# A two-layer encoder on one core: the banded heads' product with the low part of the keys over 128 rows, and where its room comes from

## The chip, the core and the metric

The kernel runs on one core of one Trainium2 chip. Its time is the device time of one execution in microseconds. TensorE (PE) multiplies, VectorE (DVE), ScalarE (ACT) and GpSimd (POOL) do the elementwise work, and SyncE (SP) issues the loads and stores.

## What is computed

An encoder of two layers over 512 tokens of width 1024, in float32. Each layer mixes tokens with three groups of heads (differential, latent, banded), attends to 256 memory tokens, and ends in a SwiGLU block; each part is normalised before and after. Cut to what matters here:

```python
for l in range(DEPTH):
    h = rmsnorm(x, g_mix_pre[l])
    (a_q, a_k, a_v, b_cq, b_ckv, b_kr, c_q, c_k, c_v) = jnp.split(h @ w_in[l], IN_SPLITS, axis=-1)
    ...
    qb = (rmsnorm(b_cq, mla_q_norm_g[l]) @ mla_w_q_up[l]).reshape(B, S, MLA_HEADS, MLA_NOPE + MLA_ROPE)
    qb = jnp.concatenate([qb[..., :MLA_NOPE], rope(qb[..., MLA_NOPE:], positions)], axis=-1)
    ...
    o_c = swa_attention(c_q.reshape(B, S, SWA_Q_HEADS, HEAD_DIM), c_k..., c_v...,
                        positions, swa_slopes, swa_sinks[l])
    mix = jnp.concatenate([o_a, o_b, o_c], axis=-1) @ w_out[l]
    x = x + rmsnorm(mix, g_mix_post[l])
    xo = cross_attention(rmsnorm(x, g_x_pre[l]), rmsnorm(mem, g_x_mem[l]), w_xq[l], w_xkv[l], w_xo[l])
```

In the banded heads (`swa_attention`) a tile of 128 queries sees its own 128 keys and the tile before and after. There are 8 query heads of 64 columns over 2 key heads.

## The kernel before, in words

Products keep nearly full float32 accuracy by splitting each operand into a high and a low part (`split`, L100 to L102: a copy that rounds on ScalarE, the remainder on VectorE) and adding three products, high by high, low by high, high by low (`mm3`, L145 to L149).

The program is written down as two streams that are woven together. The main stream is the attention in units of one head and one query tile: 16 units of differential heads, 32 of banded ones, 16 of latent ones (`chunk_units`, `diff_units`, `swa_units`, `mla_units`). Each unit is a list of stages: a score, a softmax, transposes of the weights, products with the values. The fill stream supplies TensorE with products that don't depend on attention (`fill` in `mix_phase`). Its steps there are, in the order of the string `FILL_ORDER = "qqummummukkkuu"`: "q" query columns of the banded heads, "u" one token tile of the latent heads' queries and keys (`mla_up`, with `products` and, one step later, `transposed`), "m" half a step of a memory tile's norm (`mem_norm`: load, squares, scaling; then the transposes), "k" a product of the memory with its key weights (`make_xK`). Numbers in tables set how much fill stands beside each stage. A scheduler then orders the instructions of each engine; on the chip every engine keeps that order.

The banded heads' scores are taken at L690 and L691. Keys of both key heads stand in one tile `KScV`: plane 0 and plane 1 hold the high part of head 0 and of head 1, copied to both halves of the 128 rows, and plane 2 holds the low parts, head 0 in rows 0 to 63 and head 1 in rows 64 to 127. A query tile `SQ` holds the high part in one half of the rows and the low part in the other. So L690 gives (high + low of the query) by the high part of the key in one product of 128 rows, and L691 adds the high part of the query by the low part of the key, over 64 rows. A score has 256 or 384 columns (the band is cut off at the ends).

Temporary tiles come from rings, one for each tag; `TMP_BUFS` says how many buffers a ring has. A tile that is asked for takes the next buffer of its ring, and its first writer waits for the last reader of the tile that had it. Tag "o" (2 buffers) has, around the change, the transposed values' source `cvT`, the two halves of each memory tile (L1041 loads them), and the tiles `t` in which products of the memory are collected before they are stored to DRAM (L1061). Tag "m" (3 buffers) has `qn` and `kn`, the latent heads' queries and keys of one token tile, `r5b5`, in which the rotary step of that tile is computed (L744 to L757), and the latents' norms (`latent_T`).

The memory tiles go this way: load (L1041 on SP's queue), squares on ScalarE (L199), the root on GpSimd (L203, L204), scaling on VectorE (L216), transposes on TensorE into `ps_at` (L180), split into `memTh` and `memTl` (L101, L102). Then `make_xK` multiplies.

Of the kernel before, what the change touches and what calls it, by code (L numbers as in the profile page):

```python
# [18 lines left out]
P = 128  # L19
D = 1024  # L20
KC = 8
S = 512
# [15 lines left out]
TMP_BUFS = {"e": 5, "ph": 2, "pl": 2, "o": 2, "c": 2, "m": 3}  # L38
# [10 lines left out]
def weave(main, fill, ratio):  # L49
    """Alternate the emission of two streams: `ratio` steps of fill for each step of main."""  # L50
    owed = 0.0
    done = object()
    for _ in main:
        owed += ratio
        while owed >= 1.0:
            owed -= 1.0
            if next(fill, done) is done:
                owed = -1e9
    for _ in fill:
        pass  # L60
# [9 lines left out]
def encoder_kernel(  # L70
# [16 lines left out]
    # ---------------------------------------------------------------- helpers  # L87
# [16 lines left out]
    def stage(pieces, a, b):  # L104
        """Weights from DRAM into one staging tile [P, a, b]; pieces: (partition, row chunk, column, source)."""
        st = stp.tile([P, a, b], F32, tag="st", name="st")
        for p0, k0, c, src in pieces:
            n, k, m = src.shape
            nc.sync.dma_start(st[p0:p0 + n, k0:k0 + k, c:c + m], src)
        return st  # L110

    def unit(st_view):
        """Staged weights [P, a, b] as a list of a (high, low) operands [P, b]."""
        a, b = st_view.shape[1], st_view.shape[2]
        per = 512 // b
        out_ = []
        for k0 in range(0, a, per):
            k1 = min(k0 + per, a)
            hi = wp.tile([P, k1 - k0, b], F32R, tag="wh", name="wh")
            lo = wp.tile([P, k1 - k0, b], F32R, tag="wl", name="wl")  # L120
            split(hi, lo, st_view[:, k0:k1, :])
            out_ += [(hi[:, k, :], lo[:, k, :]) for k in range(k1 - k0)]
        return out_
# [8 lines left out]
    def defer(n, i, *fns):  # L132
        """Emit fns, which belong to token tile i, n ticks later."""
        late.extend((ticks[0] + n, i, f) for f in fns)
# [24 lines left out]
    class Split8:  # L159
        """A [P, 8, n] operand as exact high and low parts, in 4-chunk slots."""  # L160
# [15 lines left out]
    def to_T(src_half, dst, half, t0, name):  # L176
        """Transpose a [P, 512] half of a token tile into chunks 4*half.. of dst, split."""
        pt = psum("at")
        for c in range(4):
            nc.tensor.transpose(pt[:, c * P:(c + 1) * P], src_half[:, c * P:(c + 1) * P], ident)  # L180
        ptv = pt.rearrange("p (c t) -> p c t", c=4)
        k0 = 4 * half
        for j in range(4 // min(4, dst.per)):
            w = min(4, dst.per)
            s = (k0 + j * w) // dst.per
            o = (k0 + j * w) % dst.per
            hi = dst.hi[s][:, o:o + w, t0:t0 + P]
            lo = dst.lo[s][:, o:o + w, t0:t0 + P]
            with tc.high_priority(offset=HASTE):
                split(hi, lo, ptv[:, j * w:(j + 1) * w, :])  # L190

    def sq_mean(halves, dst, t0, name):
        """Mean of squares over the 1024 columns given as two halves, plus EPS, to the power -1/2; the squares pass
        through dst's place for the token tile at t0."""
        ms = small(2, name + "ss")
        w = min(4, dst.per)
        for j, hv in enumerate(halves):
            k = 4 * j % dst.per
            nc.scalar.activation(dst.hi[4 * j // dst.per][:, k:k + w, t0:t0 + P],  # L199
                                 hv.rearrange("p (c t) -> p c t", t=P), AF.Square, scale=1.0 / 32.0,  # L200
                                 accum_out=ms[:, j:j + 1])
        r = small(1, name)
        nc.gpsimd.tensor_scalar(out=r, in0=ms[:, 0:1], scalar1=ms[:, 1:2], scalar2=EPS, op0=ALU.add, op1=ALU.add)  # L203
        nc.gpsimd.tensor_tensor(out=r, in0=r, in1=neghalf[:, :1], op=ALU.pow)  # L204
        return r

    def norm_to_T(halves, g, dst, t0, name, hs, spread=False):
        """rmsnorm with gain g into hs; returns the transposes into dst. spread: the first half off the vector engine."""
# [15 lines left out]
    def post_norm(i, a0, a1, g, dst, spread=False):  # L224
        """x += rmsnorm of the two halves a0, a1 with gain g. spread: the first half's gain off the vector engine."""
# [15 lines left out]
    # ---------------------------------------------------------------- setup  # L241
# [35 lines left out]
    cos2 = cp.tile([P, NT, 32], F32, tag="cos2", name="cos2")  # L277
# [15 lines left out]
    def setup():  # L293
# [16 lines left out]
        # positions in exact 16-bit halves, as rows and as columns  # L310
# [19 lines left out]
    def setup_rest():  # L330
# [13 lines left out]
        # rotary angles, reduced to [-pi, pi] by exact products of short pieces  # L344
# [46 lines left out]
        nc.scalar.activation(cos2[:, :, 0:16], cang, AF.Sin)  # L391
        nc.vector.tensor_copy(out=cos2[:, :, 16:32], in_=cos2[:, :, 0:16])
        nc.vector.tensor_scalar(out=sin2[:, :, 0:16], in0=sin2[:, :, 16:32], scalar1=-1.0, scalar2=None, op0=ALU.mult)

    # ---------------------------------------------------------------- pieces of a layer
    def transpose_pair(es, k0, k1):
        """Chunks k0..k1 of two tiles of weights -> split [128 keys, chunk, 2 x 128 queries]."""
        pt = psum("at")
        for k in range(k0, k1):
            for j, e in enumerate(es):  # L400
                c = 2 * (k - k0) + j
                nc.tensor.transpose(pt[:, c * P:(c + 1) * P], e[:, k * P:(k + 1) * P], ident)  # L402
        n = 2 * P * (k1 - k0)
        hi, lo = tmp("ph", (P, n), F32R), tmp("pl", (P, n), F32R)
        split(hi, lo, pt[:, :n])
        return [(hi[:, 2 * P * j:2 * P * (j + 1)], lo[:, 2 * P * j:2 * P * (j + 1)]) for j in range(k1 - k0)]

    def split_v(dst, src):
        """Values of two heads [P, ..., 2, 64] -> [P, ..., high 0, low 0, low 1, high 1]."""
# [3 lines left out]
    def ws_chunk(ps, u, hT, t0, t1):  # L413
        """Weight-stationary product: ps[:, t0:t1] = (128 weight columns).T @ hT[:, t0:t1]."""
# [3 lines left out]
    def as_tile(ps, us, aT, t0, n, ks=tuple(range(KC)), first=True, last=True, ticks_=False):  # L418
        """Activation-stationary product: ps[:, :n] = aT[:, t0:t0+128].T @ weights, over row chunks ks."""
# [6 lines left out]
    def nat_units(w, cols):  # L426
        """Natural-layout weights, all eight row chunks."""
# [41 lines left out]
    # ---------------------------------------------------------------- layers  # L469
# [3 lines left out]
    def mix_phase(l, head):  # L473
# [12 lines left out]
        KS_cV = slot("Sq", [P, 5, S], F32R, "KScV")  # L486
        KS, cV = KS_cV[:, 0:3, :], KS_cV[:, 3:5, :].rearrange("p a (k b d) -> p (a k) b d", b=4, d=64)
# [8 lines left out]
        # ---- projections of the mixing block  # L496
# [13 lines left out]
        def in_swa_kv():  # L510
# [6 lines left out]
            nc.vector.tensor_tensor(out=KS[up, 2, :], in0=ps[up], in1=KS[up, 1, :].bitcast(F32), op=ALU.subtract)  # L517
# [33 lines left out]
        # ---- attention as units of one head and one query tile, each a list of stages  # L551
# [6 lines left out]
        # two units (rows of the same values) share their products with the values; four such units fill half the  # L558
        # rows of an output chunk, eight the chunk
        nop = lambda *a: None  # L560

        def chunk_units(first, soft2, pairs, vals, ends):
            """pairs: per 64-row half, two (unit, unit, key chunks); vals(b, k): stationary values;
            ends: stages on the finished chunk [128, 512]."""
# [43 lines left out]
        def diff_units(c, q3, mdst):  # L608
            """The sums s0 of the first weights stay out of the products: rmsnorm(o / s0) has EPS * s0 ** 2 for EPS."""
# [68 lines left out]
        def swa_units(cp_, ip, mdst):  # L678
            """Heads 2 cp_ and 2 cp_ + 1 of both groups, query tiles 2 ip and 2 ip + 1."""
            def score(u, a, bic):  # L680
                b, i, c = bic
                pr = slice(64 * b, 64 * (b + 1))
# [8 lines left out]
                nc.tensor.matmul(ps[:, :wd], lhsT=q[pr], rhs=KS[pr, 2, c0:c0 + wd], start=False, stop=True)  # L691
# [36 lines left out]
        # ---- latent attention  # L728
        def mla_up(qT, kT, mV):
# [5 lines left out]
            def products(i):  # L735
# [8 lines left out]
                r5b5 = tmp("m", (P, 2, 5, 32))  # L744
# [10 lines left out]
                nc.vector.tensor_tensor(out=r5, in0=r5, in1=cos2[:, i:i + 1, :].to_broadcast([P, 5, 32]), op=ALU.mult)  # L755
# [46 lines left out]
        # ---- emission  # L802
# [37 lines left out]
        def early():  # L840
            """Weights of the steps after this phase, into slots of their own, ahead of the ring."""
# [56 lines left out]
    def latent_T(l, ps, a, n, scale, gl, latT, c0, i):  # L898
        """rmsnorm of ps[:, a:a+n] with gain gl, transposed and split into latT[:, :, c0:..., tile i]."""
# [15 lines left out]
    class Head:  # L915
        """The first products of a layer: the query latents, by token tile, and the first differential heads."""
# [46 lines left out]
    def out_proj(w, aT, wrow, done):  # L963
        """natural = aT.T @ w, by halves of the columns; done(i, half0, half1) takes a finished token tile."""
# [26 lines left out]
    def out_first(w, aT, accs):  # L991
        """First half of the columns of the mixing output, without the latent heads' rows (chunks 2 and 3)."""
# [10 lines left out]
    def out_late(w, aT, st_):  # L1003
        """What is left of the mixing output: st_ takes the weights and the open products of the second half."""
# [77 lines left out]
    def x_attn(l, hT, first):  # L1082
# [44 lines left out]
        def unit_(hd, tp):  # L1127
            """One head, two token tiles."""
# [220 lines left out]
```

## Time and profile before

| | |
|---|---|
| median of 3 runs | 1622.77 us (1622.03 to 1624.49) |
| span of the profiled execution | 1622.5 us |
| TensorE busy | 1579.8 us, 8225 products |
| VectorE busy | 984.2 us |
| ScalarE busy | 806.5 us |
| GpSimd busy | 119.7 us |
| DMA | 167.37 MB, mean 103 GB/s |

The profiled execution's span, from the first to the last instruction, stands for its own time; it lies 0.3 us under the median of the runs. In the page's slices TensorE is at nine tenths or more from the second slice to the last but one, and its granted clock is at full speed in all of them at the page's resolution. A matmul's duration in the trace includes the way through the array, so products in a row overlap; how fast they follow each other is read from their starts. The row "x2" or "x4" merges neighbours of the same kind. A number in brackets behind a row is idle time of that engine just before it, and what ended it.

### The profile page before, as it was taken

To read this page: it belongs to the slowest core of one execution; us is meant where nothing else is said; L and a number is where in the kernel's file an instruction comes from. 1 tells how busy PE (TensorE), PEld (TensorE's weight loads), DVE (VectorE), ACT (ScalarE), POOL (GpSimd) and SP (SyncE) were. 2 spreads that over 40 slices of the span, in tenths; PEclk is the share of its full clock that TensorE was granted. 3 is DMA by queue.
4 is the path that set the end of the run, shared out by engine and by line. 5 is a ranking of instruction groups with operands and counts; after the bars stand their busy time and mean duration, and the time that the engine had idled before them with its cause. 6 is when DMAs were issued, how large, how long until landed. Compare 5 with 4: busy or idle time off the path is not lost.

```text
span 1622.5 us, 21890 instructions
## 1 busy us (share of the span) xinstructions
PE 1579.8 (97%) x8225; PEld 1315.0 (81%) x8225; DVE 984.2 (61%) x1912; ACT 806.5 (50%) x1749; POOL 119.7 (7%) x208
## 2 busy tenths in 40 slices
PE   6999999999999999999999999999999999999998
PEld 6887877799888888888888878777888888888886
DVE  6899776665562554444566987767547434445544
ACT  5578778554553222322356787875445433222222
POOL 3101000300310000000130000003004000000000
PEclk9999999999999999999999999999999999999999
DMA  5632641241233323233245234512312423233221
GB/s 174 153 90 82 204 136 48 77 146 63 78 130 104 104 78 104 78 108 101 89 126 121 68 118 157 162 40 80 129 53 91 142 92 104 78 104 105 78 79 52
DMA packets 130010, 167.37 MB, mean 103 GB/s; under 512 B 21744, under 2 KB 100720, under 8 KB 129136
## 3 DMA queue, kind: packets, MB, share of 16 engines
q1 hardware_dynamic: 129904, 165.97, 32.8%
q8 instruction: 65, 1.06, 0.3%
q14 instruction: 41, 0.34, 0.1%
HBM read 150.22 MB, written 9.44 MB: 98 GB/s over the span
## 4 chain that ended last, share of the span: by engine, by line
PE 90%; DVE 3%; POOL 2%; ACT 2%; issue 1%; DMA 1%; SPq 0%; DVEq 0%; POOLq 0%; ACTq 0%
PE ps_mm L147 14%; PE ps_mm L149 14%; PE ps_mm L148 14%; PE ps_av L149 6%; PE ps_av L148 6%; PE ps_av L147 6%; PE ps_sc L149 5%; PE ps_sc L148 5%; PE ps_sc L147 5%; PE ps_at L402 3%; PE ps_av L573 2%; PE ps_av L574 1%; PE ps_sc L784 1%; PE ps_sc L691 1%; PE ps_at L180 1%
## 5 line engine op out<-in xcount | busy, mean ns | idle before, releaser
L102 DVE TENSOR_TENSOR wl<-st,wh 128x512 fp32r<-128x512 f32 (+1 forms) x406 | 279.4, 700 | 245.6 <-ACT wh L101 242.7
L101 ACT CAST wh<-st 128x512 fp32r<-128x512 f32 (+1 forms) x406 | 243.0, 615 | 304.1 <-PE ps_mm L148 132.6
L149 PE MATMUL ps_mm<-hfh,wl 128*128 128x512 f32 (+1 forms) x384 | 144.5, 376 | 2.5 <-DVE wl L102 2.5
L149 PE MATMUL ps_av<-hfh,wl 128*128 128x512 f32 (+1 forms) x384 | 144.3, 376 | 1.7 <-DVE wl L102 1.7
L147 PE MATMUL ps_mm<-hfh,wh 128*128 128x512 f32 (+1 forms) x384 | 144.4, 376 | 0.6 <-ACT hfh L101 0.6
L148 PE MATMUL ps_mm<-hfl,wh 128*128 128x512 f32 (+1 forms) x384 | 144.6, 377 | 0.0
L147 PE MATMUL ps_av<-hfh,wh 128*128 128x512 f32 (+1 forms) x384 | 144.3, 376 | 0.0
L148 PE MATMUL ps_av<-hfl,wh 128*128 128x512 f32 (+1 forms) x384 | 144.3, 376 | 0.0
L147 PE MATMUL ps_sc<-dwh,f 128*128 128x512 f32 x320 | 124.8, 390 | 0.0
L149 PE MATMUL ps_sc<-dwh,f 128*128 128x512 f32 x320 | 124.6, 389 | 0.0
L148 PE MATMUL ps_sc<-dwl,f 128*128 128x512 f32 x320 | 124.6, 389 | 0.0
L101 ACT CAST dwh<-st 128x1024 fp32r<-128x1024 f32 x40 | 40.0, 1047 | 157.6 <-PE ps_sc L149 153.4
L102 DVE TENSOR_TENSOR pl<-ps_at,ph 128x512 fp32r<-128x512 f32 (+1 forms) x128 | 82.7, 654 | 25.1 <-ACT ph L101 24.1
L149 PEld LDWEIGHTS ps_mm<-hfh,wl 128*128 128x128 f32 x384 | 72.0, 188 | 17.7 <-DVE wl L102 3.0
L149 PEld LDWEIGHTS ps_av<-hfh,wl 128*128 128x128 f32 x384 | 72.0, 187 | 16.8 <-DVE wl L102 2.1
L101 ACT CAST ph<-ps_at 128x512 fp32r<-128x512 f32 (+1 forms) x128 | 70.6, 562 | 29.8 <-PE ps_at L402 28.2
L147 PEld LDWEIGHTS ps_mm<-hfh,wh 128*128 128x128 f32 x384 | 72.0, 187 | 15.7 <-ACT hfh L101 1.1
L148 PEld LDWEIGHTS ps_mm<-hfl,wh 128*128 128x128 f32 x384 | 72.0, 188 | 15.2 <-DVE hfl L102 0.4
L147 PEld LDWEIGHTS ps_av<-hfh,wh 128*128 128x128 f32 x384 | 72.0, 188 | 14.7
L148 PEld LDWEIGHTS ps_av<-hfl,wh 128*128 128x128 f32 x384 | 72.0, 188 | 14.6
L402 PE MATMUL ps_at<-ident,e 128*128 128x128 f32 x480 | 77.2, 275 | 3.3 <-DVE memTl L102 2.2
L203 POOL TENSOR_SCALAR rpost<-rpostss 128x1 f32<-128x1 f32 x24 | 9.0, 375 | 932.0 <-ACT hTh L199 716.1
(363 smaller groups left out, 3896.4 us busy)
## 6 DMA issues: line engine op xcount, KB each, us to landing
st<-in_w_ffn_in SPq DMA_DIRECT2D x44, 1024.0 KB, 5.1
st<-in_w_ffn_out SPq DMA_DIRECT2D x22, 1024.0 KB, 4.9
st<-in_w_xkv SPq DMA_DIRECT2D x16, 1024.0 KB, 5.6
st<-in_w_out SPq DMA_DIRECT2D x16, 512.0 KB, 5.0
st<-in_w_xq SPq DMA_DIRECT2D x8, 1024.0 KB, 5.2
st<-in_w_xo SPq DMA_DIRECT2D x8, 1024.0 KB, 5.4
st<-in_w_in SPq DMA_DIRECT2D x12, 512.0 KB, 4.1
q<-stg SPq DMA_DIRECT2D x48, 128.0 KB, 2.4
```

The costliest lines, as they stand in the source:

```text
L101: nc.scalar.copy(hi, src)
L102: nc.vector.tensor_tensor(out=lo, in0=src, in1=hi.bitcast(F32), op=ALU.subtract)
L147: nc.tensor.matmul(ps, lhsT=lh, rhs=rh, start=first, stop=False)
L148: nc.tensor.matmul(ps, lhsT=lh, rhs=rl, start=False, stop=False)
L149: nc.tensor.matmul(ps, lhsT=ll, rhs=rh, start=False, stop=last)
L180: nc.tensor.transpose(pt[:, c * P:(c + 1) * P], src_half[:, c * P:(c + 1) * P], ident)
L203: nc.gpsimd.tensor_scalar(out=r, in0=ms[:, 0:1], scalar1=ms[:, 1:2], scalar2=EPS, op0=ALU.add, op1=ALU.add)
L402: nc.tensor.transpose(pt[:, c * P:(c + 1) * P], e[:, k * P:(k + 1) * P], ident)
L573: nc.tensor.matmul(av, lhsT=v, rhs=hi, start=k == u["k0"], stop=False)
L574: nc.tensor.matmul(av, lhsT=v, rhs=lo, start=False, stop=k == u["k1"] - 1)
L691: nc.tensor.matmul(ps[:, :wd], lhsT=q[pr], rhs=KS[pr, 2, c0:c0 + wd], start=False, stop=True)
L784: nc.tensor.matmul(ps, lhsT=mla["qT"][:, h, i * P:(i + 1) * P], rhs=mla["kT"][:, h, :], start=True, stop=True)
```

## The change

There are four edits. (1) The low parts of the keys get a plane for each key head, with the other half of the rows zero; `KScV` grows from 5 planes to 6, and GpSimd fills the zero halves in each layer. (2) L691 takes the whole query tile and the key head's plane, all 128 rows. The half of the query tile that holds low parts meets zeros, so the result is the same sum. (3) `r5b5` comes from ring "o" in place of "m", and "m" has 2 buffers in place of 3. (4) The cosine table is kept once, for 16 columns, and read twice by a view. Comments are also removed, which moves line numbers by a few. The core of the diff:

```diff
-TMP_BUFS = {"e": 5, "ph": 2, "pl": 2, "o": 2, "c": 2, "m": 3}
+TMP_BUFS = {"e": 5, "ph": 2, "pl": 2, "o": 2, "c": 2, "m": 2}
...
-    cos2 = cp.tile([P, NT, 32], F32, tag="cos2", name="cos2")
+    cos1 = cp.tile([P, NT, 16], F32, tag="cos1", name="cos1")
...
-        nc.scalar.activation(cos2[:, :, 0:16], cang, AF.Sin)
-        nc.vector.tensor_copy(out=cos2[:, :, 16:32], in_=cos2[:, :, 0:16])
+        nc.scalar.activation(cos1, cang, AF.Sin)
...
-        KS_cV = slot("Sq", [P, 5, S], F32R, "KScV")
-        KS, cV = KS_cV[:, 0:3, :], KS_cV[:, 3:5, :].rearrange("p a (k b d) -> p (a k) b d", b=4, d=64)
+        KS_cV = slot("Sq", [P, 6, S], F32R, "KScV")
+        KS, cV = KS_cV[:, 0:4, :], KS_cV[:, 4:6, :].rearrange("p a (k b d) -> p (a k) b d", b=4, d=64)
...
             nc.vector.tensor_tensor(out=KS[lo, 2, :], in0=ps[lo], in1=KS[lo, 0, :].bitcast(F32), op=ALU.subtract)
-            nc.vector.tensor_tensor(out=KS[up, 2, :], in0=ps[up], in1=KS[up, 1, :].bitcast(F32), op=ALU.subtract)
+            nc.vector.tensor_tensor(out=KS[up, 3, :], in0=ps[up], in1=KS[up, 1, :].bitcast(F32), op=ALU.subtract)
+            nc.gpsimd.memset(KS[up, 2, :].bitcast(F32), 0.0)
+            nc.gpsimd.memset(KS[lo, 3, :].bitcast(F32), 0.0)
...
-                pr = slice(64 * b, 64 * (b + 1))
...
-                nc.tensor.matmul(ps[:, :wd], lhsT=q[pr], rhs=KS[pr, 2, c0:c0 + wd], start=False, stop=True)
+                nc.tensor.matmul(ps[:, :wd], lhsT=q, rhs=KS[:, 2 + b, c0:c0 + wd], start=False, stop=True)
...
-                r5b5 = tmp("m", (P, 2, 5, 32))
+                r5b5 = tmp("o", (P, 2, 5, 32))
...
-                nc.vector.tensor_tensor(out=r5, in0=r5, in1=cos2[:, i:i + 1, :].to_broadcast([P, 5, 32]), op=ALU.mult)
+                r5h = r5.rearrange("p h (a d) -> p h a d", a=2)
+                nc.vector.tensor_tensor(out=r5h, in0=r5h, in1=cos1[:, i:i + 1, :].unsqueeze(1).to_broadcast([P, 5, 2, 16]),
+                                        op=ALU.mult)
```

The scheduler gives some engines another order. SP's queue in the first layer before, from the latent heads' weights to the first store of xK (`in_mem` is the memory, `in_w_xkv` its weights, `gains` a norm's gains):

```order
L109 DMA st<-in_mla_w_q_up 128x2x384
L1041 DMA o<-in_mem 128x512 x2
L923 DMA glat<-in_mla_q_norm_g 128x256
L924 DMA glat<-in_mla_kv_norm_g 128x128
L109 DMA st<-in_mla_w_kv_up 128x512
L109 DMA st<-in_w_xkv 128x8x256
L238 DMA gains<-in_g_x_mem 128x1024
L109 DMA st<-in_w_xkv 128x8x256
L1041 DMA o<-in_mem 128x512 x2
L109 DMA st<-in_w_xkv 128x8x256
L1061 DMA xK_dram<-o 128x512
L109 DMA st<-in_w_xkv 128x8x256
```

and with the change:

```order
L109 DMA st<-in_mla_w_kv_up 128x512
L109 DMA st<-in_w_xkv 128x8x256
L238 DMA gains<-in_g_x_mem 128x1024
L1043 DMA o<-in_mem 128x512
L109 DMA st<-in_w_xkv 128x8x256
L1043 DMA o<-in_mem 128x512 x2
L109 DMA st<-in_w_xkv 128x8x256
L1043 DMA o<-in_mem 128x512
L109 DMA st<-in_w_xkv 128x8x256
L1063 DMA xK_dram<-o 128x512
```

The first memory tile's two halves, which stood together ahead of the weights of the memory, are now further back and apart, and so are the second tile's; the second half of the second tile stands behind the third weight load, and the first store of xK behind the fourth. The queue of the second layer has the same order.

TensorE in the first layer before, around the transposes of the first memory tile (L180; L690 and L691 are score products, L573 and L574 products with the values, L402 transposes of attention weights, L766 those of the latent heads' queries or keys):

```order
L690 MATMUL ps_sc<-KScV,SQ_548 128x256
L691 MATMUL ps_sc<-KScV,SQ_548 128x256
L574 MATMUL ps_av<-pl,aV 128x256
L573 MATMUL ps_av<-ph,aV 128x256
L574 MATMUL ps_av<-pl,aV 128x256
L180 MATMUL ps_at<-ident,o 128x128 x8
L402 MATMUL ps_at<-ident,e 128x128 x4
L766 MATMUL ps_at<-ident,m 96x128 x4
```

and with the change (lines 573 and 574 are now 574 and 575, 402 is 401):

```order
L691 MATMUL ps_sc<-KScV,SQ_548 128x256
L575 MATMUL ps_av<-pl,aV 128x256
L574 MATMUL ps_av<-ph,aV 128x256
L575 MATMUL ps_av<-pl,aV 128x256
L690 MATMUL ps_sc<-KScV,SQ_549 128x256
L691 MATMUL ps_sc<-KScV,SQ_549 128x256
L690 MATMUL ps_sc<-KScV,SQ_548 128x384
L691 MATMUL ps_sc<-KScV,SQ_548 128x384
L180 MATMUL ps_at<-ident,o 128x128 x8
L401 MATMUL ps_at<-ident,e 128x128 x4
```

Two pairs of scores have moved ahead of these transposes. Ahead of the first product with the transposed memory there are nine pairs with the change, and seven before.

## Rows read from the trace of the kernel before

**Rows 1.** The page, busy time, share of the span and instructions of each engine.

```profile
PE 1579.8 (97%) x8225; PEld 1315.0 (81%) x8225; DVE 984.2 (61%) x1912; ACT 806.5 (50%) x1749; POOL 119.7 (7%) x208
```

**Rows 2.** TensorE by line and shape, the 64-row products: count, busy us, mean ns.

```profile
L691 PE MATMUL ps_sc<-KScV,SQ 64*128 64x384 f32 x32 | 14.1, 440 | 0.0
...
L691 PE MATMUL ps_sc<-KScV,SQ 64*128 64x256 f32 x32 | 12.4, 386 | 0.0
```

**Rows 3.** TensorE in order of time: start us, duration us, line, output<-inputs, shape.

```profile
135.56 0.33 PE L690 MATMUL ps_sc<-KScV,SQ 128*128 128x384 f32 x1
135.73 0.40 PE L147 MATMUL ps_mm<-wh,latT 128*128 128x512 f32 x1
135.96 0.40 PE L148 MATMUL ps_mm<-wl,latT 128*128 128x512 f32 x1
136.20 0.39 PE L149 MATMUL ps_mm<-wh,latT 128*128 128x512 f32 x1
136.52 0.44 PE L691 MATMUL ps_sc<-KScV,SQ 64*128 64x384 f32 x1
136.89 0.44 PE L690 MATMUL ps_sc<-KScV,SQ 128*128 128x384 f32 x1
137.25 0.44 PE L691 MATMUL ps_sc<-KScV,SQ 64*128 64x384 f32 x1
137.63 0.55 PE L402 MATMUL ps_at<-ident,e 128*128 128x128 f32 x3
```

**Rows 4.** TensorE in order of time, a 96-row product among 128-row ones.

```profile
97.50 0.39 PE L622 MATMUL ps_sc<-q 96*128 96x512 f32 x1
97.74 0.39 PE L147 MATMUL ps_mm<-hTh,wh 128*128 128x512 f32 x1
```

**Rows 5.** SP's queue in order of time, loads of the memory tiles, first layer.

```profile
98.95 0.96 SPq L1041 DMA_DIRECT2D o<-in_mem  x2
...
142.95 1.05 SPq L1041 DMA_DIRECT2D o<-in_mem  x2
```

**Rows 6.** Landing us: memory loads, then issues of 100 to 200 us (count, KB, median).

```profile
DMA to landing us min/median/max: 2.8/3.2/3.9
...
st<-in_w_xkv SPq DMA_DIRECT2D x8, 1024.0 KB, 5.8
xK_dram<-o SPq DMA_DIRECT2D x4, 256.0 KB, 4.1
```

**Rows 7.** VectorE in order of time, the last adds of two rope steps.

```profile
140.48 0.28 DVE L757 TENSOR_TENSOR m<-m 128x128 f32<-128x128 f32 x1
...
150.46 0.28 DVE L757 TENSOR_TENSOR m<-m 128x128 f32<-128x128 f32 x1
```

**Rows 8.** ScalarE in order of time, the last square of memory tile 1.

```profile
147.19 0.64 ACT L199 ACTIVATE memTh<-o 128x512 fp32r<-128x512 f32 x1
```

**Rows 9.** TensorE in order of time, the memory stage of the first layer.

```profile
142.25 1.35 PE L180 MATMUL ps_at<-ident,o 128*128 128x128 f32 x8 [0.19 <-DVE sr L710]
144.71 0.66 PE L402 MATMUL ps_at<-ident,e 128*128 128x128 f32 x4 [1.11 <-DVE memTl L102]
...
149.92 0.63 PE L180 MATMUL ps_at<-ident,o 128*128 128x128 f32 x4
...
154.63 0.36 PE L147 MATMUL ps_mm<-memTh,wh 128*128 128x256 f32 x1
```

**Rows 10.** TensorE in order of time, first product with the memory, second layer.

```profile
954.50 0.38 PE L147 MATMUL ps_mm<-memTh,wh 128*128 128x256 f32 x1
```

**Rows 11.** Stretches: us; busy us of PE, PEld, DVE, ACT, POOL; granted clock; DMA; GB/s.

```profile
945.00:947.00 2.00, 1.27 (x8) 1.00 (x6) 1.77 (x4) 2.00 (x5) 0.00 (x0) 0.75 0.35 123
947.00:949.00 2.00, 2.00 (x10) 1.77 (x8) 1.49 (x7) 1.53 (x6) 0.89 (x2) 0.50 0.00 0
```

**Rows 12.** GpSimd: a fill by line and shape, and the wait before a gain, layer border.

```profile
masks.py:197 POOL MEMSET ident<- 128x128 f32 x1 | 0.2, 205 | 0.3 <-POOLq L1338 0.3
...
828.59 1.68 POOL L213 TENSOR_TENSOR c<-x,gains 128x512 f32<-128x512 f32 x1 [0.93 <-DVE x L232]
```

## The prediction

> **What bounds the kernel now.** I read the page's busy times first, then TensorE's instructions by shape and in order of time, then the queue of loads, and last who waits around the memory tiles. TensorE is busy in 97% of the span [rows 1], so a microsecond of it that is saved or lost nearly anywhere moves the end. Two places matter, and they pull in opposite directions.
>
> The first is the product that the change is named after. 32 are 384 columns wide and 32 are 256 [rows 2]. Full-height products of 384 and 512 columns follow each other at 0.17 us (135.56 to 135.73) and 0.23 us (135.73 to 135.96) [rows 3]. The 64-row product breaks this rhythm on both sides. Into it: 136.20 to 136.52 is 0.32 instead of 0.23, and 136.89 to 137.25 is 0.36 instead of 0.17. Out of it: 136.52 to 136.89 is 0.37 and 137.25 to 137.63 is 0.38, instead of 0.17. That is 0.29 and 0.40 us lost, 0.345 us on average, at each product. A product of 96 rows in a stream of 128-row ones starts the next after 0.24 us [rows 4], so a shorter contraction alone does not do it; 64 rows do.
>
> The second place is the memory stage, whose work stands in the same stretch. Its first tile is loaded at 98.95 us, long before its transposes at 142.25 us. The second tile is loaded at 142.95 us, when the transposes have freed the buffers "o", and is transposed from 149.92 us [rows 5, 9]. TensorE's order is fixed, so whatever stands behind a transpose waits for it; the products with the transposed memory start at 154.63 us.
>
> **The change, part by part.** *The 64 products.* Columns, output and weights stay; only the height of the operands grows to 128. From the 96-row case I take the plain rhythm for them, so the gain is 0.345 us each, 22 us for 64. The bounds are 0.29 and 0.40 us (18.6 and 25.6 us).
>
> Here a rule speaks against the change. The rows show 0.37 us for a 64-row product where a full one takes 0.17 us [rows 3]. The Trainium skill, page TensorEngine Tiling (Array Packing), section Overview, says instead that a contraction of 64 or less leaves the full array underused and that row tiling may be up to twice as fast, since two half-height tiles can work in parallel. By that rule the widening gives nothing, and the sum below would end 15.9 us higher. The trace does not agree: the neighbours of the half-height products are all full-height, and no two of them overlap.
>
> *The rotary buffer.* This is the edit that costs. "m" falls from three buffers to two, and r5b5 moves to "o", whose two buffers the halves of the memory tiles use. The fetch order of SP now has the second half of memory tile 0 behind the first rope step, and the second half of tile 1 behind the second one. The first rope step needs its buffer until its last add, 140.48 + 0.28 = 140.8 us [rows 7]. Then the load is issued and lands after 3.2 us (2.8 to 3.9) [rows 6]. From the start of the last square to the transposes the trace shows 147.19 to 149.92, 2.7 us [rows 8, 9]. So the transposes of tile 0 come at 140.8 + 3.2 + 2.7 = 146.7 us, not at 142.25: 4.5 us late.
>
> The second rope step then takes a buffer that these transposes free. From the first transposes to the end of the second rope step is now 142.25 to 150.75, 8.5 us [rows 7, 9]; some of that was other work between, and I take 8.0. That gives 154.7 us. Another load and square, 5.9 us, gives 160.6. A 1 MB weight load, which takes 5.8 us to land [rows 6], now stands just ahead of that load in the queue; I add 1.4 us, half of the difference to 3.2. So tile 1 is transposed at 162.0 us instead of 149.92, 12.1 us late, and so are the products with it. In the new order of TensorE two more pairs of scores stand ahead of these products (nine against seven), worth 2 x (0.17 + 0.17 + 0.345) = 1.4 us, which the wait covers. The loss is 12.1 - 1.4 = 10.7 us in a layer. The second layer has the same order, and before it has the same distance (954.50 for its first product [rows 10]), so the loss is 21.4 us. Bounds for a layer: 7 us (landing in 2.8, 6.5 instead of 8.0, nothing ahead in the queue) and 14 us (landing in 3.9, 8.5, all 2.6 us of the weight load).
>
> This also cuts the gain. Nine of a layer's 32 widened products stand in the stretch that now waits for loads, and save nothing. 46 are left: 46 x 0.345 = 15.9 us.
>
> *The clock.* In the second layer TensorE is busy for only 1.27 us of the 2 from 945 us, and the granted clock there is 0.75 and in the next 2 us 0.50 of full, the 1.2 GHz level [rows 11]. The new wait of about 6 us in one piece will do this in both layers. 3 us at half clock with work to do cost 1.5 us; the second layer pays one such dip already. I take 2.4 us for both layers together, between 0 and 6.
>
> *The last rope step* takes a buffer from which xK is being stored (4.1 us to land [rows 6]), and the store is now queued behind a weight load. VectorE stands still there, but TensorE has 24 products of 256 columns (2.8 us at half of the 0.23 us that 512 take) and the products of a rope step ahead of it, some 5 us. I take 1.0 us in all, between 0 and 6.
>
> *The rest.* Four fills of 64x512 on GpSimd: 128x128 takes 0.21 us [rows 12], so about 0.5 us each. The first two stand at the start of the program, where the first normalisation waits for the load of its gains. The next two fall into 0.93 us in which GpSimd waits for x [rows 12]; nothing, or 0.2 us. If that cover were gone each pair would cost 1 us. The cosine table with one copy keeps its 160 elements: nothing. Two "m" buffers for the latent norms: their transposes are settled one tile later, so nothing waits.
>
> **Sum.** 21.4 - 15.9 + 2.4 + 1.0 = +8.9 us on the profiled span of 1622.5 us; the median of the runs is 0.3 us above it, so 1631.7, which I give as 1632 us.
>
> **The rivals.** *The loads stay covered (faster).* If the two hops cost TensorE little, the 22 us stay: down to 1601 us. The place is the first product with the transposed memory. If it comes less than 7.7 us later than before in each layer, the 7.95 us that remain to gain, with the 1.4 us moved ahead, outweigh the wait and the 1.7 us of a layer for the clock and the last rope step. For it speaks that the second load had 7 us of which TensorE lost only 1.1 us in one piece [rows 9]; against it, that two loads are now serial with rope steps and that little is left to put between. With a delay of 4 us a layer and 1.7 us for both layers' clock and rope the time is 1622.8 + 2 x (4 - 1.4 - 7.95) + 1.7 = 1614 us. Chance 0.19.
>
> *No change that can be measured.* Within 0.2%, which is about what a measurement of this kernel can tell from no change (1619.5 to 1626.0 us), a delay of 6.1 to 9.3 us in each layer gives that by the same sum. Chance 0.15.
>
> *The widening gives nothing (slower still).* If the lost time belongs to something else that the full-height product keeps, the sum is 21.4 + 3.4 = +24.8, 1648 us. Against it speaks the 96-row product [rows 4]. Chance 0.07.
>
> *The waits are at their upper bounds (slower still).* The weight load goes ahead in full and the clock falls twice: 2 x 13 - 15.9 + 6 + 3 = +19, 1642 us and above. Chance 0.12.
>
> **How the numbers follow.** The forecast, slower by 3 to 16 us, has 0.47. Slower in all is 0.47 + 0.07 + 0.12 = 0.66; the same 0.15; faster 0.19. The range leaves out the lower half of the faster case and what lies above 1645 us, about 2 in 10: 1612 to 1645 us. Slower cases alone hold 1626 to 1645.
>
> **What would show it.** Right: the product at L691 at 128 rows, with the next instruction 0.17 us behind it at 384 columns; the transposes at L180 of the memory tiles in the stretch behind 130 us some 5 and 12 us later than now; a wait of TensorE of several us ahead of the second one, ended by VectorE's "o"; a granted clock of 0.5 behind it in both layers; about 16 us less elsewhere in the two stretches of the banded heads. Wrong: memory products that start within 6 us of their old place, or gaps of 0.3 us around the widened products.

## The result, and the profile after

The change made the kernel slower: 1635.62 us (median of four runs, 1633.53 to 1638.26) against 1622.43 us for the kernel before beside it. The ratio is 1.0083 with a 95% interval of 1.0067 to 1.0100. The profiled execution after took 1633.65 us with a span of 1631.9 us; its span is 9.4 us above that of before, the medians are 13.2 us apart. The profile shows an execution near the lower end of the four.

The page's busy times come first, to be read beside [rows 1].

```profile
PE 1567.6 (96%) x8225; PEld 1318.6 (81%) x8225; DVE 984.1 (60%) x1911; ACT 805.9 (49%) x1749; POOL 121.9 (7%) x212
```

TensorE issued the same 8225 products and was busy for 12.2 us less, in a span that is 9.4 us longer. So it stands still about 21.6 us more than before. Products became cheaper and something else took more than they gave. The product that was widened stands in the view of TensorE by line and shape (count, busy us, mean ns, idle before):

```profile
L691 PE MATMUL ps_sc<-KScV,SQ 128*128 128x384 f32 x32 | 11.7, 366 | 0.0
L691 PE MATMUL ps_sc<-KScV,SQ 128*128 128x256 f32 x32 | 9.0, 280 | 0.0
```

Beside [rows 2] the mean fell from 440 to 366 ns and from 386 to 280 ns. What counts is how soon the next product starts. TensorE in order of time after (start, duration, line, output<-inputs, shape), to be read beside [rows 3]:

```profile
135.16 0.33 PE L690 MATMUL ps_sc<-KScV,SQ 128*128 128x384 f32 x1
135.33 0.34 PE L691 MATMUL ps_sc<-KScV,SQ 128*128 128x384 f32 x1
135.50 0.34 PE L690 MATMUL ps_sc<-KScV,SQ 128*128 128x384 f32 x1
135.68 0.34 PE L691 MATMUL ps_sc<-KScV,SQ 128*128 128x384 f32 x1
135.85 0.49 PE L401 MATMUL ps_at<-ident,e 128*128 128x128 f32 x3
```

Every start is 0.17 us behind the one before. The gaps of 0.3 and 0.4 us around the 64-row product are gone, as forecast.

Where the lost time stood before is in the rows of the weight loads (PEld) of the kernel before, for the same stretch as [rows 3]:

```profile
135.97 0.19 PEld L149 LDWEIGHTS ps_mm<-wh,latT 128*128 128x128 f32 x1
136.51 0.18 PEld L691 LDWEIGHTS ps_sc<-KScV,SQ 64*128 64x128 f32 x1 [0.36 <-issue]
136.88 0.19 PEld L690 LDWEIGHTS ps_sc<-KScV,SQ 128*128 128x128 f32 x1 [0.19 <-DVE m L748]
```

The weights of the full-height product that starts at 136.20 are loaded from 135.97, while the product before it (start 135.96) runs. The weights of the 64-row product are loaded only from 136.51, 0.01 us ahead of its own start, and so are those of the full-height product behind it (136.88 against 136.89). In the trace of before this is so for all 64 products and for those right behind them: there the load is not hidden behind the product before. With the change most of these loads begin 0.1 us or more ahead of their product again.

The loss stands in the memory stage. SP's queue in order of time, first layer, after; compare [rows 5]:

```profile
139.48 8.86 SPq L1043 DMA_DIRECT2D o<-in_mem  x2
153.06 0.38 SPq L109 DMA_DIRECT2D st<-in_w_xkv  x1
154.82 0.33 SPq L1043 DMA_DIRECT2D o<-in_mem  x1
```

The first row is two loads. The second half of tile 0 is issued at 139.48 us, where before both halves had been issued at 98.95. The last half of tile 1 goes out at 154.82 us, 1.8 us behind a 1 MB weight load. VectorE and ScalarE in order of time say why, and what follows (in brackets: idle time just before, and what ended it):

```profile
154.47 0.28 DVE L759 TENSOR_TENSOR m<-o 128x128 f32<-128x128 f32 x1
...
159.30 0.63 ACT L199 ACTIVATE memTh<-o 128x512 fp32r<-128x512 f32 x1 [4.18 <-DMA o<-in_mem]
...
161.10 1.42 DVE L216 SCALAR_TENSOR_TENSOR o<-o,rmem,gains 128x512 f32<-128x512 f32 x2 [5.48 <-POOL rmem L204]
...
181.13 0.18 DVE L748 COPY o<-kr 128x32 f32<-128x32 f32 x1 [0.61 <-DMA xK_dram<-o]
```

The last add of the second rope step ends at 154.75 us and frees the buffer; 0.07 us later the load is issued; 4.5 us after that ScalarE can square it; then root and scaling, and the transposes start at 161.91. The last row is the rope step that takes a buffer from which xK is being stored: VectorE waits 0.61 us for it, and TensorE does not stand still there.

TensorE through the memory stage, first layer, then the same places of the second; compare [rows 9, 10]:

```profile
146.04 1.94 PE L180 MATMUL ps_at<-ident,o 128*128 128x128 f32 x8 [3.23 <-DVE o L216]
...
161.91 1.97 PE L180 MATMUL ps_at<-ident,o 128*128 128x128 f32 x8 [6.34 <-DVE o L216]
...
167.51 0.56 PE L147 MATMUL ps_mm<-memTh,wh 128*128 128x256 f32 x1
167.87 0.41 PE L148 MATMUL ps_mm<-memTl,wh 128*128 128x256 f32 x1
168.08 0.41 PE L149 MATMUL ps_mm<-memTh,wl 128*128 128x256 f32 x1
...
950.90 1.94 PE L180 MATMUL ps_at<-ident,o 128*128 128x128 f32 x8 [3.14 <-DVE o L216]
...
966.70 1.97 PE L180 MATMUL ps_at<-ident,o 128*128 128x128 f32 x8 [6.10 <-DVE o L216]
```

There are two waits in each layer where before there was none of this kind but the one at the program's start. The eight transposes take 1.94 us in place of 1.35, and products of 256 columns follow at 0.21 us where the plain rhythm is 0.12: TensorE has half its clock here. The view of stretches of 2 us (busy us of PE, PEld, DVE, ACT, POOL, then the granted clock, DMA) shows it:

```profile
140.00:142.00 2.00, 0.51 (x2) 0.30 (x2) 2.00 (x9) 1.95 (x5) 0.00 (x0) 1.00 0.38 131
142.00:144.00 2.00, 0.75 (x2) 0.30 (x2) 1.31 (x5) 1.92 (x7) 0.17 (x1) 0.60 0.00 0
...
150.00:152.00 2.00, 2.00 (x9) 1.91 (x8) 2.00 (x8) 2.00 (x8) 0.00 (x0) 0.50 0.07 25
...
156.00:158.00 2.00, 0.00 (x0) 0.00 (x0) 0.00 (x0) 0.00 (x0) 0.00 (x0) 1.00 1.10 382
...
166.00:168.00 2.00, 2.00 (x11) 1.61 (x10) 0.70 (x3) 2.00 (x7) 0.00 (x0) 0.50 0.00 0
```

From 156 to 158 us no engine works and the DMA engines are full: the weights and the memory half arrive together. In the first wait and behind both the clock stands at 0.50, the 1.2 GHz level, and TensorE is fully busy at it from 150 to 152 and from 166 to 168 us. The first fall is not the work of the 3.23 us wait alone: a share of 0.60 for 142 to 144 us puts it at about 142.4, and this wait begins at 142.81 (146.04 - 3.23). From 140 to 142 us TensorE had been busy for 0.51 of 2 us at the full clock, since its score products waited for VectorE. Before, the first layer had no slice at half clock here.

The sum over the program is in the list of TensorE's waits (us in total, times, longest), after:

```profile
PE ps_at L180 <- DVE o L216: 29.0, 5, 10.2
...
PE ps_sc L690 <- DVE snm L693: 3.6, 4, 1.0
```

and before:

```profile
PE ps_at L180 <- DVE o L216: 10.3, 1, 10.3
```

The one wait of 10.3 us is the program's start. So the memory tiles cost 29.0 - 10.2 = 18.8 us of waits, in four pieces, beside the 3.6 us for scores, which the list of before does not have.

### The profile page after: what moved, and what is told of

It reads as the page before. It is cut to its first block, busy times and chain, and to the rows that moved or that the text cites. A ratio compares the mean times of both kernels' runs of the same rounds, so it can differ in the third digit from the quotient of the medians.

```text
span 1631.9 us, 21877 instructions
## 1 busy us (share of the span) xinstructions
PE 1567.6 (96%) x8225; PEld 1318.6 (81%) x8225; DVE 984.1 (60%) x1911; ACT 805.9 (49%) x1749; POOL 121.9 (7%) x212
## 4 chain that ended last, share of the span: by engine, by line
PE 84%; DVE 3%; ACT 3%; POOL 2%; DMA 2%; issue 1%; DVEq 0%; POOLq 0%; ACTq 0%; SPq 0%
PE ps_mm L147 13%; PE ps_mm L149 13%; PE ps_mm L148 13%; PE ps_av L149 6%; PE ps_av L148 6%; PE ps_av L147 6%; PE ps_sc L149 5%; PE ps_sc L147 5%; PE ps_sc L148 5%; PE ps_at L401 3%; PE ps_sc L786 2%; PE ps_av L574 1%; PE ps_av L575 1%; PE ps_at L180 1%; PE ps_sc L623 1%
```

## The experiments

The theory after the result: the widening gains what the gaps around the product show, the rotary buffer in ring "o" makes the loads of the memory serial with the rope steps, and this costs waits and clock. One such chain of rope step, load and square is called a hop; a layer has two. The first four kernels take these apart.

**Room of its own for the rotary buffer.** `room` is here the tile of the gains, made twice as large. In the rows of some of these kernels line numbers are a few higher than in the change.

```diff
-                r5b5 = tmp("o", (P, 2, 5, 32))
+                r5b5 = room()[:, 1, 320 * (i % 3):320 * (i % 3 + 1)].rearrange("p (a h d) -> p a h d", a=2, h=5)
...
-            g, = gains("H3", g_x_mem[l])
+            g = room()[:, 0, :]
+            nc.sync.dma_start(g, g_x_mem[l].unsqueeze(0).to_broadcast([P, D]))
```

> The change whole, except that r5b5 stands neither in ring "o" nor in "m" but in room of its own: the gains of the memory's norm take a tile of twice their size, and its second half holds r5b5 in three places in turn. "m" keeps 2 buffers, the product keeps 128 rows. Theory (the widening gains about 22 us over the whole program, the buffer in "o" costs all that was lost, everything else nothing): 1601 us, 1598 to 1605; SP's loads of the memory in their old order, transposes of the memory tiles at about 142 and 150 us again. Rival A (the widening gives nothing): 1622 us. Rival B (the two buffers of "m", the fills or the cosine table cost part of it): 1606 to 1620 us.

1607.7 us, ratio 0.9912 (0.9898 to 0.9925): 14 us faster than the kernel before and 28 faster than the change. The memory stage is back in its old place, as these rows of TensorE show:

```profile
141.39 1.35 PE L180 MATMUL ps_at<-ident,o 128*128 128x128 f32 x8 [0.20 <-DVE sr L710]
...
148.77 0.60 PE L180 MATMUL ps_at<-ident,o 128*128 128x128 f32 x4
```

The time lies above the theory's range, in that of rival B. The third kernel decides between them.

**The product over 64 rows again,** in the changed kernel.

```diff
-                nc.tensor.matmul(ps[:, :wd], lhsT=q, rhs=KS[:, 2 + b, c0:c0 + wd], start=False, stop=True)
+                nc.tensor.matmul(ps[:, :wd], lhsT=q[pr], rhs=KS[pr, 2 + b, c0:c0 + wd], start=False, stop=True)
```

> The changed kernel with one edit undone: L691 runs over 64 rows of the new planes again. The order of every engine is that of the changed kernel. Theory: the products in the waiting stretch hide their lost time, the others show it, 46 x 0.345 to 64 x 0.345 us: 1635.6 + 16 to 22 = 1652 to 1658 us. Rival A (the widening gives nothing): 1635.6 us, within 2 us.

1649.0 us, ratio 1.0170 (1.0156 to 1.0184). Undoing the widening costs 13.4 us. Rival A falls; but the size is under the theory's lower end of 16. In the profiled executions the two kernels are further apart, 15.3 us (spans of 1631.9 and 1647.2 us), so the 13.4 us are uncertain by some 2 us.

**Both.** The two edits above in one kernel.

> Both together: r5b5 in room of its own and L691 over 64 rows; what is left of the change are the sixth plane and its fills, the single cosine table and two buffers in "m". The order of every engine is that of the run with room of its own and 128 rows. Theory (the rest costs nothing): 1622 us, 1620 to 1625. Rival B (the rest costs): 1626 us and more. The difference to the run with 128 rows is the widening alone without waits: 22 us (18.6 to 25.6) by theory, 0 by rival A.

1623.21 us, ratio 1.0013 (1.0004 to 1.0021). Plane, fills, cosine table and the smaller ring "m" cost 1.4 us by the medians (0.6 to 3.4 us by the interval): little, but not shown to be nothing. So rival B does not explain the 1607.7 us: the widening without waits is worth 1623.2 - 1607.7 = 15.5 us and not 22. These two kernels have the same order on every engine, so their traces can be laid side by side, product by product. With 128 rows:

```profile
162.91 0.34 PE L690 MATMUL ps_sc<-KScV,SQ 128*128 128x384 f32 x1
163.08 0.34 PE L691 MATMUL ps_sc<-KScV,SQ 128*128 128x384 f32 x1
163.26 0.28 PE L147 MATMUL ps_mm<-memTh,wh 128*128 128x256 f32 x1
...
1020.74 0.40 PE L148 MATMUL ps_mm<-wl,mixT 128*128 128x512 f32 x1
...
1034.54 0.39 PE L574 MATMUL ps_av<-ph,mV 128*128 128x256 f32 x1 [1.26 <-ACT ph L101]
```

With 64 rows, the same products:

```profile
165.49 0.33 PE L691 MATMUL ps_sc<-KScV,SQ 128*128 128x384 f32 x1
165.75 0.44 PE L692 MATMUL ps_sc<-KScV,SQ 64*128 64x384 f32 x1
166.13 0.38 PE L147 MATMUL ps_mm<-memTh,wh 128*128 128x256 f32 x1
...
1038.22 0.50 PE L148 MATMUL ps_mm<-wl,mixT 128*128 128x512 f32 x1
...
1050.51 0.38 PE L574 MATMUL ps_av<-ph,mV 128*128 128x256 f32 x1
```

The three starts take 0.17 and 0.18 us with 128 rows, 0.26 and 0.38 us with 64: 0.09 into the product and 0.20 out of it, 0.29 in all. That is mostly the case: 46 of the 64 products lose 0.27 to 0.30 us in all. Only four, where the pair of scores stands directly behind another pair, lose 0.19 or more on the way in; the rest stand near waits, at half clock, or where the kernel with 128 rows is itself slower. Summed over the 64 from the starts in both traces the difference is 17.2 us. At the end of the second layer's banded heads the lead is 17.5 us (1020.74 against 1038.22), and then some is given back: TensorE now comes early to the first latent heads and waits 1.26 us for ScalarE's copy of their weights, where the slower kernel did not wait. At that product the lead is 16.0 us. Behind this wait the kernel with 128 rows runs at half clock (0.50) for a while, which the other does not; its view of stretches:

```profile
1036.00:1038.00 2.00, 2.00 (x11) 2.00 (x11) 0.73 (x3) 1.58 (x5) 0.00 (x0) 0.50 0.00 0
```

By 1038.8 us the lead is down to 14.6 us; at the end it is 15.0 us.

**Products without use in the second wait,** to hold the clock up. This is the changed kernel with, ahead of the transposes of tile 1 in each layer:

```diff
+        if name == "rmem" and half == 0:
+            KS = state["KS"]
+            for _ in range(0 if t0 == 0 else 24):
+                nc.tensor.matmul(pt, lhsT=KS[:, 0, 0:P], rhs=KS[:, 0, 0:512], start=True, stop=True)
```

> The changed kernel with 24 products of 512 columns, whose results are not used, ahead of the transposes of the second memory tile in each layer; 24 x 0.23 = 5.6 us, a little less than TensorE's wait there (6.3 and 6.1 us). Theory (the half clock behind this wait costs what the profile of the changed kernel shows: about 7 us of work at half speed, 3.5 us in each layer): the clock stays at full behind this wait and the time falls to 1628.6 us (1627 to 1631). Rival C (only the wait costs, the half clock hides under further waits, or it falls all the same): 1635 to 1637 us.

1633.3 us, ratio 1.0069 (1.0056 to 1.0081), against 1.0083 (1.0067 to 1.0100) for the change: the intervals overlap, so by the times it is open whether anything was won. The time lies between the theory's range and that of rival C. The trace says more:

```profile
152.71 5.82 PE L182 MATMUL ps_at<-KScV 128*128 128x512 f32 x24
...
161.77 1.38 PE L184 MATMUL ps_at<-ident,o 128*128 128x128 f32 x8 [1.15 <-DVE o L220]
...
172.72 0.36 PE L579 MATMUL ps_av<-ph,KScV 128*128 128x256 f32 x1
...
194.46 0.66 PE L405 MATMUL ps_at<-ident,e 128*128 128x128 f32 x4 [2.44 <-ACT e L560]
```

The same places in the changed kernel:

```profile
174.99 0.36 PE L574 MATMUL ps_av<-ph,KScV 128*128 128x256 f32 x1
...
195.12 0.66 PE L401 MATMUL ps_at<-ident,e 128*128 128x128 f32 x4 [0.76 <-ACT e L555]
```

In the first layer the transposes start where they did (161.77 against 161.91) and take 1.38 us instead of 1.97. Behind the memory products TensorE is 2.27 us early (172.72 against 174.99), 0.14 us of it already at the transposes: some 2.1 us is what the half clock behind the second wait cost, under the 3.5 us expected. By 194.46 it waits 2.44 us for ScalarE's scaled weights, where it waited 0.76 us, and most of the lead is gone. In the second layer the products of the same kind held the clock only through the wait. It fell about 2.5 us after the transposes began (at 966.17 us), behind short waits of 0.65 and 0.82 us, as the view of stretches shows:

```profile
970.00:972.00 2.00, 2.00 (x11) 1.77 (x10) 1.09 (x5) 1.89 (x7) 0.00 (x0) 0.50 0.00 0
```

The 1.5 us won there were lost in a wait of 1.89 us for the latent heads' weights (0.46 us in the changed kernel). So the half clock is a cost in its place, and what it gives back is for a good part covered later.

**Tile 1 out of the ring.** The changed kernel, r5b5 still in "o"; `room` is a slot of 8 KB (H1) that holds nothing between the last use of the layer's input and the second chunk of the banded heads' output.

```diff
-                    m = tmp("o")
+                    m = room()[:, 0, 512 * j:512 * (j + 1)] if t else tmp("o")
```

> The changed kernel, with the second memory tile's two halves in room that is free in this stretch (slot H1) in place of ring "o"; r5b5 stays in "o", so the first memory tile's second half still waits behind the first rope step. Theory (two serial hops of rope step, load and square, each exposed): the second wait of TensorE (6.3 and 6.1 us) goes with the half clock behind it (2.2 us in the first layer by the run with dummy products), the first of 3 us and its half clock stay: 1635.6 - 12.4 - 4 = 1619 us, 1616 to 1623. Rival D (the whole loss comes from the first hop, the second is its echo): 1631 us and more.

1618.75 us, ratio 0.9978 (0.9969 to 0.9987): the second hop costs 16.9 us, as expected, and rival D falls. TensorE shows the first hop unchanged and the second without a wait, though still at half clock from the first (four transposes in 1.05 us where the kernel with room for r5b5 takes 0.60):

```profile
146.71 1.94 PE L180 MATMUL ps_at<-ident,o 128*128 128x128 f32 x8 [3.15 <-DVE o L216]
...
153.61 1.05 PE L180 MATMUL ps_at<-ident,room 128*128 128x128 f32 x4
```

The rest of the way to the kernel with room for r5b5 is 1618.8 - 1607.7 = 11.1 us. That kernel also loads tile 1 otherwise; the next one differs from this one in the place of r5b5 alone and is 1618.8 - 1605.6 = 13.2 us faster, which is the price of the first hop of both layers.

**Room for both,** r5b5 and tile 1.

```diff
-                r5b5 = tmp("o", (P, 2, 5, 32))
+                r5b5 = room()[:, 1, 320 * (i % 3):320 * (i % 3 + 1)].rearrange("p (a h d) -> p a h d", a=2, h=5)
...
-                    m = tmp("o")
+                    m = room()[:, 0, 512 * j:512 * (j + 1)] if t else tmp("o")
```

> The changed kernel, with both r5b5 (three places in turn) and the second memory tile in room that is free in this stretch (slot H1, 8 KB of a partition). Neither hop is left, and the second tile's load no longer waits for the first tile's transposes, as it did in the kernel before. By theory it beats the run with room for r5b5 alone (1607.7 us) by the waits still in its memory stage, some 3.5 us in the first layer and 3.9 in the second by the busy times of its stretches, if other work fills them: 1602 us, 1600 to 1607. Rival E (those waits are of VectorE's and ScalarE's chain and not of the load): 1606 to 1609 us.

1605.57 us, ratio 0.9899 (0.9886 to 0.9913), the fastest of the kernels; 2.1 us under room for r5b5 alone, with intervals that overlap. By the time it lies in the theory's range, 0.4 us under the lower end of rival E's. By the trace rival E is nearer: the first product with the memory starts at 154.87 us, with room for r5b5 alone at 155.16, so the load was not what held the stage, and where the 2.1 us come from stays open.

**Another order of the fill steps,** nothing else:

```diff
-FILL_ORDER = "qqummummukkkuu"
+FILL_ORDER = "qqmmmmuuukkkuu"
```

> The changed kernel with another order of the fill steps and nothing else: both memory tiles ahead of all rope steps. In ring "o" the memory tiles then follow each other, tile 1 waits only for the transposes of tile 0, and no load stands behind a rope step. Theory: one hop is left, with fewer products to cover it than in the kernel before: 1613 us, 1606 to 1622. Rival F (the rope steps that now wait for tile 1's buffers expose as much): 1630 to 1640 us.

1617.43 us, ratio 0.9974 (0.9961 to 0.9986): 18 us better than the change without one byte more, slightly above the value expected. Rival F falls. One hop is left, and it is short:

```profile
147.04 1.94 PE L180 MATMUL ps_at<-ident,o 128*128 128x128 f32 x8 [1.56 <-DVE o L216]
```

**The 64-row product twice in a row,** in the kernel before. The low part of the keys enters the scores twice, so it computes something else.

```diff
+                nc.tensor.matmul(ps[:, :wd], lhsT=q[pr], rhs=KS[pr, 2, c0:c0 + wd], start=False, stop=False)
                 nc.tensor.matmul(ps[:, :wd], lhsT=q[pr], rhs=KS[pr, 2, c0:c0 + wd], start=False, stop=True)
```

> The kernel before, in which each 64-row product is issued twice in a row (the low part of the keys enters the scores twice). Theory (the lost time belongs to the change between products of 128 and of 64 rows, so a second 64-row product behind the first costs its plain rhythm of 0.17 or 0.12 us): 32 x (0.17 + 0.12) = 9.3 us more, 1631 us, 1629 to 1634. Rival G (each 64-row product loses its time on its own): 9.3 + 64 x 0.3 = 28 us more, 1650 us, 1645 to 1655.

1632.89 us, ratio 1.0070 (1.0057 to 1.0083), 10.7 us more: the theory's 9.3 us, not rival G's 28. TensorE:

```profile
136.12 0.34 PE L690 MATMUL ps_sc<-KScV,SQ 128*128 128x384 f32 x1
136.39 0.44 PE L691 MATMUL ps_sc<-KScV,SQ 64*128 64x384 f32 x1
136.67 0.33 PE L692 MATMUL ps_sc<-KScV,SQ 64*128 64x384 f32 x1
136.93 0.45 PE L690 MATMUL ps_sc<-KScV,SQ 128*128 128x384 f32 x1
```

The starts are 0.27, 0.28 and 0.26 us apart. Three products of 384 columns in plain rhythm are 0.51 us and here take 0.81: 0.30 us lost for the two together, as much as for one alone. So a group of 64-row products pays about once, whether it has one or two. The theory does not hold border by border, though: the second 64-row product does not follow in its plain 0.17 us but loses 0.11 too, and the way back costs 0.09 instead of 0.20 us.

## Why the prediction came out as it did

The sign, the mechanism and the range (1612 to 1645 us) were right; the forecast of 1632 us was 3.6 us low. By its own steps, with the medians of the runs:

*The rotary buffer.* This step held nearly to the number, in part by luck. Transposes of tile 0 were forecast at 146.7 us and came at 146.04; the second rope step was to end at 154.7 and ended at 154.75; tile 1 was forecast at 162.0 and came at 161.91; the first product with the memory at 166.7, and it came at 167.51. Errors cancelled on the way: the first rope step let its buffer go at 139.4 and not at 140.8 us, the way from load to transposes took 6.6 instead of 5.9 us, and the stretch to the end of the second rope step 8.7 instead of 8.0. With the product over 64 rows the whole move cost 1649.0 - 1623.2 = 25.8 us, forecast 21.4 + 2.4 + 1.0 = 24.8 us. With the product over 128 rows it cost 1635.6 - 1607.7 = 27.9 us.

*The clock.* Both layers were to lose 2.4 us in all, with 6 as the upper bound, from one dip of 3 us with work in each. There were two dips in each layer, one at each hop; the first began in the first layer just before the 3.2 us wait, while score products waited, which the prediction had not counted. Behind the second alone the first layer lost some 2.1 us and the second about 1.5, where 1.5 and less were taken for a dip; each stretch at half clock held some 7 us of work and not 3. So the step had both the number of dips and the price of one too low. How much of it reaches the end was not settled: most of what the products without use won was lost again in the next waits.

*The 64 products.* This term was mis-sized. The step took 0.345 us for each, the mean of two neighbours of which the second, 0.40 us, came directly behind another pair [rows 3]. Only four of 64 stand like that; most lose 0.27 to 0.30 us, about the lower bound given. That makes 17.2 us and not 22, and 15.5 at the program's end. In the changed kernel 13.4 us were left by the medians, 15.3 by the profiled executions, forecast 15.9. What the waits swallow, forecast as 6 of 22 us, is thus not settled at the end of the program; in the memory stage itself the traces bear the step out in part, since behind the second wait only about 1.0 us of what the nine products lose is left in each layer. The 96-row product [rows 4] as the nearest row for a product without loss was well chosen.

*The rule* of the Trainium skill, page TensorEngine Tiling (Array Packing), section Overview, is that row tiling may be up to twice as fast for a contraction of 64 or less. No run here works on two half-height tiles at once, so that is not tested. What the prediction took from it, that the widening gives nothing, fell: the runs with 64 and with 128 rows differ by 13.4 and 15.5 us.

*The last rope step* was given 1.0 us; 0.61 and 0.44 us on VectorE in the two layers and nothing on TensorE is what the trace shows. *The rest* was given nothing and came out at 1.4 us (0.6 to 3.4).

Together, 25.8 - 13.4 + 1.4 = 13.8 us, against a forecast of 8.9 and 13.2 between the medians. The shortfall of 4.9 us is 2.5 for the gain, 1.0 for the move with its clock, 1.4 for the rest. Each of these is uncertain by one or two us, so this split is rough.

## What to carry to other kernels

When an edit needs room, read who else takes turns in the ring that pays for it: a small temporary put between prefetched loads turns two early loads into a chain of load, work, load. An order of steps in which the loads of a ring follow each other leaves one short hop, and a slot that is dead in that stretch gives the room without any, as the runs at 1617.4 and 1605.6 us show. And a 64-row product among 128-row ones cost about 0.29 us here, while a 96-row one cost nothing [rows 4]: so look for the weight load that starts only with its product, and then either widen the product, or put several of that height together.

## What the runs showed that was not expected

The lost time around 64 rows is not tied to one product: two in a row lost 0.10, 0.11 and 0.09 us at their three borders, one alone 0.09 and 0.20, in both cases about 0.30 us. It goes with weight loads that start only when their own product does. In the pair the second product's load starts 0.18 us ahead of it (136.49 against 136.67) and is hidden in part. Why the height decides this, no run shows.

The gain from faster products does not arrive in full even in a kernel that keeps TensorE busy for 97% of its span: 17.2 us were won at the products and 15.0 us reached the end, because ScalarE's weights for the first latent heads then came too late, and the wait for them was followed by a stretch at half clock.

A wait costs twice: the waits for scores and for the tile, of which the last took 3.2 us, were followed by eight transposes in 1.94 us instead of 1.35. And filling a wait with products does not secure the clock for what follows: in the first layer it stayed at full speed, in the second the same 24 products held it through the wait and it was halved shortly after.
